# One PSUM tile for the whole kernel, and the last two modulation blocks taken as a pair

## The chip, the cores and the metric

The kernel runs on one core of a Trainium2 chip. The metric is the device time of one execution in microseconds; the median of 3 runs before the change is 1285.03 us (1284.46 to 1285.83). The engines are named as the profile names them: PE (TensorE, matmuls), PEld (its weight loads), DVE (VectorE), ACT (ScalarE), POOL (GpSimd), SP (SyncE, which here only issues transfers).

## What is computed

One layer of a diffusion backbone on 512 tokens of width 2048, with 256 context tokens, cut to what matters here:

```python
shift, scale, gate = split(silu(c) @ w_ada + b_ada, 3)      # 2048 x 6144, one vector each
h = rmsnorm(x, norm_g) * (1 + scale) + shift                # 512 x 2048
p = h @ w_in                                                # 2048 x 9216: q, k, v, z_a, u_b, z_b, g_a, g_b
y_b = (fourier_mix(p[u_b]) * silu(p[z_b])) @ w_pb           # a 2-D FFT, real part, per group of 128 channels
y_a = (attention(q, k, v) * silu(p[z_a])) @ w_pa            # keys and values of the context are appended
out = rmsnorm(x + gate * ((sigmoid(p[g_a]) * y_a + sigmoid(p[g_b]) * y_b) @ w_out), final_g)
```

All is float32. A product is made as three matmuls: each operand is split into a high part and a low remainder (both float32r), and `mm3` (L336 to L340) adds high x high, high x low and low x high into one PSUM bank. A split (`split_from`, L180) is one ACT copy (L181) and one DVE subtraction (L182).

## The kernel before

**Stages.** First comes a start stage, in which the 16 blocks of 128 channels of `h` (the rows `hhi[k]`, `hlo[k]`, 128 channels x 512 tokens each) are made one after another and are used at once for the columns u_b and z_b of `w_in`. The Fourier mixing follows (`tokens`, `positions`, L938 to L963). Then eight groups of 512 x 1024 products of the remaining columns of `w_in` (class `Group`, each of seven products P1, Q5, P2, Q6, P7, Q3, Q4), then attention with the product of `w_pb` filled in between, then the branch and output products.

**How a block of `h` is modulated.** For block k, `modulate(k)` (L573) takes a bank from `bank2` and issues 32 small matmuls (`matvec`, L562: 16 blocks of `c` against a 256-column piece of `w_ada`, on 128 x 32 of the array each, L566). ACT copies the sums out (`taken`, L593). `turned` (L595) transposes them with two matmuls into the other half of the bank (L598). `factors` (L608) adds the quarters with one DVE reduction (L613) and makes gain and shift (L619, L621). `make_h` (L647) scales the row on DVE (L650), makes the high part on ACT (L651) and the low part on DVE (L653). `modulate_pair` (L580) does two blocks in one bank: 64 small matmuls, where the second block's use `c` moved by two columns, then one ACT copy, one pair of transposes and one reduction for both.

**The order in the start stage.** The program writes the order of PE by hand (`manual_schedule(engines={E.PE})`, L796), and until L901 that of ACT and DVE too (L803). The products of the stage come from a generator, `start_work` (L681); `some(n)` takes n of its steps. `STEPS` (L41) says what they are. From block 4 on blocks go in twos: eight steps of one `mm3` (three matmuls of 512 columns) for u_b, the first four with the first block's row, the next four with the second's; then four steps of two `mm3` for z_b. For blocks 12 to 15 it is eight steps of u_b for 12 and 13, then eight for 14 and 15, then z_b of all four. Each u_b piece accumulates in four banks of `bank`; z_b pieces go through the two banks of `bank3` and are added by DVE (L679).

The loop at L863 modulates blocks 6 and 7, 8 and 9, 10 and 11, 12 and 13 in pairs. After the pair 12 and 13 come four steps. The loop at L892 then takes block 14 (two steps, `modulate(14)`, one step, its row) and block 15 (three steps, `modulate(15)`, one step, its row). Row 14 is first used in the ninth step after that loop begins, row 15 in the thirteenth. The pieces of `w_ada` come through SP (`wada_load`, L492): two transfers of 1 MB for a block, into four buffers. The two of block 15 are issued behind the pair 12 and 13.

**PSUM.** There are eight banks. Until the Fourier mixing ends they belong to a pool `ps` with three kinds of tile: `bank` (four), `bank2` (two), `bank3` (two). This pool is closed at L989. The groups then take tiles of two banks from a pool `psp` (`pair`, L1025): tag x with two buffers, y0 and y1. `psp` is closed at L1479, and one tile `whole_psum` with all eight banks follows (L1481), of which attention and all behind it use slices: `wide` for the scores, bank 6 for the products that are filled in (`fill_acc`), bank 7 for the values. A pool that says `reuse_waits="tile"` makes a new tile wait for those old tiles that lie where it lies. Inside one tile an instruction waits for earlier ones that touch the same bank.

**Behind the start stage** the order is not written by hand, except where `issue_after` says so: the compiler's scheduler orders each engine's instructions. The hand-written order of PE ends with the Fourier mixing (L981). `positions(g)` (L950) takes two banks of `bank` for each of four groups: ACT copies the second out (L960), and DVE reads the first twice (L961, L962). The next PE work is P1 of group 0: for each of four pieces of weights two 128-channel blocks times two token blocks t = 0, 1, one bank each (L1101 to L1106).

Of the kernel before, what the change touches and what calls it, by code (L numbers as in the profile page):

```python
# [10 lines left out]
F32 = mybir.dt.float32  # L11
# [4 lines left out]
PSUM = bass.MemoryType.PSUM  # L16
DRAM = bass.MemoryType.DRAM

P = 128
# [3 lines left out]
KK = D // P  # L23
# [100 lines left out]
def block_kernel(ctx, tc, xT, ctx_rows, ctx_toks, x, c_row, w_ss, w_gate, vecs, qkg, rope, dft_c, dft_s,  # L124
# [4 lines left out]
    def region(name, side="left", **kw):  # L129
        st = ExitStack()  # L130
        return st, st.enter_context(tc.tile_pool(name=name, bufs=1, side=side, **kw))
# [18 lines left out]
    b_d = dsc.tile([2, P, 2, T], F32, name="b_d")  # L150
    g_d = dsc.tile([2, 2, 4, P, 1024], F32, name="g_d")
    yb_d = dsc.tile([2, 4, P, 1024], F32, name="yb_d")
    pss, ps = region("ps", None, space=PSUM)

    cnt = [0]

    def uid(s):
        cnt[0] += 1
        return f"{s}{cnt[0]}"
# [8 lines left out]
    def hm_tile(shape, dt, name):  # L168
        return slot(hm, shape[1:], dt)

    def bank(shape=(P, 512)):
        return ps.tile(list(shape), F32, tag="b1", bufs=4, name=uid("pb"))

    def bank2():
        return ps.tile([P, 512], F32, tag="b2", bufs=2, name=uid("pd"))

    def bank3():
        return ps.tile([P, 512], F32, tag="b3", bufs=2, name=uid("pc"))

    def split_from(src, hi, lo):  # L180
        first = nc.scalar.activation(hi, src, ACT.Copy)  # L181
# [302 lines left out]
    def load_start():  # L484

        may[0] = 1
        with tc.issue_after(last_load[0]):
            load_more()
        assert not may[0]
        last_load[0] = asked[0].ins  # L490
# [82 lines left out]
    def modulate(kb, meanwhile=lambda: None):  # L573
        two[kb] = bank2()
        for h in range(2):
            matvec(kb, h)
        meanwhile()
        return taken(kb)

    def modulate_pair(kb, loads):  # L580
        two[kb] = two[kb + 1] = bank2()
        for i in range(2):
            for h in range(2):
                matvec(kb + i, h, i == 0, i == 1)
            if i:
                taken(kb)
            wada.pop(kb + i, None)
            loads(kb + i)
# [13 lines left out]
    def columns(kb):  # L602
        turned(kb)
        factors(kb)
# [42 lines left out]
    def make_h(kb, meanwhile=lambda: None):  # L647
        rows_of(kb)
        v = xt[:, kb, :]
        nc.vector.scalar_tensor_tensor(v, v, gain[:, kb, 0:1], rx if kb else rx0[0], op0=ALU.mult, op1=ALU.mult)  # L650
        act = nc.scalar.activation(hhi[kb], v, ACT.Identity, bias=shift[:, kb, 0:1])  # L651
        meanwhile()
        return nc.vector.scalar_tensor_tensor(hlo[kb], v, shift[:, kb, 0:1], hhi[kb].bitcast(F32),  # L653
                                              op0=ALU.add, op1=ALU.subtract), act

    def form_row(j):

        a, b = xt[:, j, :], xt[:, j + 8, :]
        h, i = divmod(j, 4)
        d = pap.tile([P, 1], F32, tag="d", bufs=2, name=uid("d"))  # L660
        nc.vector.tensor_tensor(d, shift[:, j, 0:1], shift[:, j + 8, 0:1], op=ALU.subtract)
        nc.vector.tensor_tensor(whole["S3", h][:, i, :], a[:, :256], a[:, 256:], op=ALU.subtract)
        nc.vector.scalar_tensor_tensor(whole["Z5", h][:, i, :], a[:, 256:], d, b[:, 256:], op0=ALU.add, op1=ALU.subtract)
# [74 lines left out]
    def some(n):  # L738
        for _ in range(n):
            next(work)  # L740
# [24 lines left out]
    def split_next():  # L765
        e = next(e for e in ahead if e.out is None and e.kind != "raw")
        split_piece(e)
        e.raws = []
# [27 lines left out]
    with tc.manual_schedule(engines={E.PE}):  # L796
        warm(8, ones)
        norms = token_norms()
        two[0] = bank2()
        matvec(0, 0)  # L800
        rx0.append(spread(*norms))
        matvec(0, 1)
        with tc.manual_schedule(engines={E.Activation, E.DVE}):  # L803
            nc.scalar.copy(rx, rx0[0])
            by_root(0)
            split_next()
            taken(0)
            wada[2] = wada_load(2)
            load_start()
            columns(0)  # L810
            row_hi(0)
            scaled(0)
            row_lo(0)
            split_next()
            by_root(1)
            some(4)
            modulate(1)
            rest = split_hi()
            wada[3] = wada_load(3)
            load_start()  # L820
            some(1)
            columns(1)
            some(1)
            row_hi(1)
            rest()
            scaled(1)
            row_lo(1)
            some(2)
            for kb in range(1, 4):
                k = kb + 1  # L830
                some(2 + (kb == 1))
                by_root(k)
                modulate(k, split_next)
                if kb < 3:
                    wada[k + 2] = wada_load(k + 2)
                    load_start()
                hold()
                some(2 - (kb == 1))
                columns(k)
                row_hi(k)  # L840
                release()
                scaled(k)
                if kb < 3:
                    some(2)
                row_lo(k)
                if kb == 3:
                    some(2)
                    by_root(5)
                    modulate(5)
                    for k in (6, 7):  # L850
                        wada[k] = wada_load(k)
                        load_start()
                    hold()
                    some(2)
                    columns(5)
                    row_hi(5)
                    release()
                    scaled(5)
                    load_rope()
                    row_lo(5)  # L860
                else:
                    some(2)
            for kb in range(4, KK - 4, 2):  # L863
                some(3)
                split_next()
                some(5)
                split_next()
                if kb == 6:
                    rotations()
                k = kb + 2  # L870

                def loads(k):
                    wada[k + 2] = wada_load(k + 2)
                    for _ in range(2 if k + 2 == KK - 3 else 1):
                        load_start()

                modulate_pair(k, loads)
                some(1)
                turned(k)
                factors(k)  # L880
                make_h(k, lambda: some(1))
                factors(k + 1)
                make_h(k + 1, lambda: some(1))
                if k >= 8:
                    form_row(k - 8)
                    form_row(k - 7)
                some(1)
                if kb == KK - 6:
                    split_table(0)
                    split_from(get(("dftc", 0)), fch[:, 0, :], fch[:, 1, :])  # L890
                    load_start()
            for k in (KK - 2, KK - 1):  # L892
                some(2 if k < KK - 1 else 3)
                modulate(k)
                some(1)
                columns(k)
                make_h(k)
                split_next()
                if k < KK - 1:
                    load_start()  # L900
                form_row(k - 8)  # L901
        some(1)
        some(8)
    may[0], asks[0] = 1 << 30, nc.sync
    while next(work):
        pass
# [79 lines left out]
    pst.close()  # L986


    pss.close()  # L989
    fm2 = ctx.enter_context(tc.tile_pool(name="fm2", bufs=1, reuse_waits="tile"))  # L990
    fms = [fm] * 4 + [fm2] * (KK - 4)
    turn_fm = [4]
    evs, evp = region("evp", "right", reuse_waits="tile")
    new_ev = lambda: evp.tile([P, 2, 512], F32, tag="ev", bufs=4, name=uid("ev"))
    qzs, qzp = region("qzp", "right", reuse_waits="tile")
    pgs, psp = region("psp", None, space=PSUM, reuse_waits="tile")
    last_y = [0]

    banks = []
    rows4 = lambda hi, lo: [(hi[:, j, :], lo[:, j, :]) for j in range(4)]  # L1000

    def make_form(f, h):
# [22 lines left out]
    def pair(tag, skip=0):  # L1025
        if isinstance(tag, int):
            return banks[0][:, tag : tag + 2, :] if tag < 6 else banks[1]
        if banks:
            last_y[tag == "x"] += 1
            b = 2 * (last_y[tag == "x"] % 2) + (4 if tag == "y" else 0)  # L1030
            return banks[0][:, b : b + 2, :] if b < 6 else banks[1]
        if tag == "y":
            last_y[0] += 1 + skip
            return psp.tile([P, 2, 512], F32, tag=f"y{last_y[0] % 2}", bufs=1, name=uid(tag))
        return psp.tile([P, 2, 512], F32, tag=tag, bufs=2, name=uid(tag))


    forms = {"A11": [(hhi[j][:, :256], hlo[j][:, :256]) for j in range(8)],
# [437 lines left out]
    ats_, atp = region("atp", "right", reuse_waits="tile")  # L1476


    pgs.close()  # L1479
    psq = ctx.enter_context(tc.tile_pool(name="psq", bufs=1, space=PSUM, reuse_waits="tile"))  # L1480
    whole_psum = psq.tile([P, 8, 512], F32, name="banks")  # L1481
    banks += [whole_psum[:, :6, :], whole_psum[:, 6:, :]]
    last_y[:] = [0, 0]
    wide = [flat(banks[0])[:, NKEY * i : NKEY * i + NKEY] for i in range(4)]
    fill_acc, b1 = banks[1][:, 0, :], lambda: banks[1][:, 1, :]
# [605 lines left out]
```

## Time and profile before

| | |
|---|---|
| median of 3 runs | 1285.03 us |
| profiled execution: its time, its span | 1286.17 us, 1284.4 us |
| PE busy | 1269.6 us, 99% |
| DVE, ACT, POOL busy | 77%, 53%, 14% |
| DMA moved | 319.07 MB, mean 248 GB/s |
| instructions | 17614 |

The page of the profile gives busy time by engine and the chain of work that ended last. The timeline lists single instructions: start, duration, engine, line, what is written from what; at the end in brackets how long the engine sat idle before it and what ended that. Matmuls are pipelined: one of 512 columns is shown with 0.39 us, but the next starts about 0.23 us after it. PEld and the bracket of a matmul are therefore read together, and a delay of PE is read from the starts of successive matmuls. In the windows view a row gives busy time by engine in one stretch, and PEclk, the granted clock of TensorE as a share of full speed. In names, pd is a bank of `bank2`, pc of `bank3`, pb of `bank`; ado is the copied sums, wa a piece of `w_ada`.

### The profile page before, as it was taken

Reading aid. Unit: us, or ns where it says so; the run is one execution under the profiler, and the core shown is the slowest. Engines: PE = TensorE matmul, PEld = TensorE weight load, DVE = VectorE, ACT = ScalarE, POOL = GpSimd, SP = SyncE. Lnnn points to the kernel's source line nnn. Section 1 sums busy time; section 2 is a strip of 40 time slices with the busy share of each in tenths; the row PEclk is TensorE's granted clock in tenths of the full one; section 3 lists DMA queues with packets and bytes.
Section 4 is the critical chain, followed back from the end, with each engine's and each line's share of the span. In section 5 each row is a group of like instructions: output and inputs, shape, how many; then the busy total and the mean of one; then the engine's idle time right before and its main releaser. Section 6 shows DMA issues by size and latency. Waiting matters only on the chain.

```text
span 1284.4 us, 17614 instructions
## 1 busy us (share of the span) xinstructions
PE 1269.6 (99%) x6554; PEld 1045.1 (81%) x6554; DVE 989.9 (77%) x1302; ACT 680.9 (53%) x1073; POOL 175.9 (14%) x229
## 2 busy tenths in 40 slices
PE   8999999999999999999999999999999999999997
PEld 5677888888888888888888888888888888788886
DVE  5767899889778787748687656788798777787677
ACT  5322765555456464443354545666677646465544
POOL 0000121111102011012031010021100221211310
PEclk8999999999999999999999999999999999999999
DMA  9998798888898998877879797588762989998986
GB/s 377 405 374 346 244 205 254 229 240 234 236 306 222 299 288 258 290 199 181 285 200 309 234 253 234 174 240 264 250 191 82 249 240 257 247 200 232 218 209 181
DMA packets 104422, 319.07 MB, mean 248 GB/s; under 512 B 9968, under 2 KB 32880, under 8 KB 100368
## 3 DMA queue, kind: packets, MB, share of 16 engines
q1 hardware_dynamic: 54336, 195.24, 42.1%
q0 software_dynamic: 27680, 100.29, 36.8%
q10 hardware_dynamic: 22320, 22.42, 5.1%
q8 instruction: 51, 0.84, 0.2%
q14 instruction: 35, 0.29, 0.1%
HBM read 283.30 MB, written 34.61 MB: 248 GB/s over the span
## 4 chain that ended last, share of the span: by engine, by line
PE 96%; DMA 1%; DVE 1%; ACT 1%; issue 1%; POOL 0%; SPq 0%; DVEq 0%; ACTq 0%
PE banks L338 11%; PE banks L340 10%; PE banks L339 10%; PE x L339 9%; PE x L340 9%; PE x L338 9%; PE y L339 8%; PE y L340 8%; PE y L338 8%; PE banks L1570 3%; PE pd L566 2%; PE pc L338 1%; PE pb L338 1%; PE pc L340 1%; PE pc L339 1%; PE pb L339 1%
## 5 line engine op out<-in xcount | busy, mean ns | idle before, releaser
L181 ACT ACTIVATE whi<-R 128x1024 fp32r<-128x1024 f32 x138 | 145.3, 1058 | 141.7 <-PE banks L340 49.3
L182 DVE TENSOR_TENSOR wlo<-R,whi 128x1024 fp32r<-128x1024 f32 x138 | 168.0, 1223 | 58.9 <-ACT whi L181 58.9
L182 DVE TENSOR_TENSOR wlo<-wr,whi 128x1024 fp32r<-128x1024 f32 (+1 forms) x122 | 147.5, 1215 | 64.5 <-ACT whi L181 64.4
L181 ACT ACTIVATE whi<-wr 128x1024 fp32r<-128x1024 f32 (+1 forms) x122 | 127.2, 1050 | 119.9 <-PE y L340 36.2
L338 PE MATMUL banks<-whi,s 128*128 128x512 f32 (+1 forms) x400 | 157.1, 393 | 0.7 <-ACT ev L1179 0.7
L340 PE MATMUL banks<-whi,s 128*128 128x512 f32 (+1 forms) x400 | 156.3, 391 | 0.0
L339 PE MATMUL banks<-wlo,s 128*128 128x512 f32 (+1 forms) x400 | 156.1, 390 | 0.0
L339 PE MATMUL x<-wlo,s 128*128 128x512 f32 x352 | 137.1, 389 | 0.2 <-DVE wlo L182 0.2
L338 PE MATMUL x<-whi,s 128*128 128x512 f32 x352 | 137.1, 390 | 0.0
L340 PE MATMUL x<-whi,s 128*128 128x512 f32 x352 | 137.0, 389 | 0.0
L291 POOL DMA_DIRECT2D R<-in_w_g x68 | 59.3, 873 | 481.5 <-DVE wlo L182 219.9
L339 PE MATMUL y<-wlo,s 128*128 128x512 f32 x316 | 123.2, 390 | 0.0
L338 PE MATMUL y<-whi,s 128*128 128x512 f32 x316 | 123.0, 389 | 0.0
L340 PE MATMUL y<-whi,s 128*128 128x512 f32 x316 | 122.8, 389 | 0.0
L181 ACT ACTIVATE s<-wr 128x512 fp32r<-128x512 f32 (+2 forms) x93 | 60.4, 676 | 67.0 <-DMA wr<-cf_d 23.9
L182 DVE TENSOR_TENSOR s<-wr,s 128x512 fp32r<-128x512 f32 (+2 forms) x93 | 66.9, 752 | 31.4 <-ACT s L181 30.4
L338 PEld LDWEIGHTS banks<-whi,s 128*128 128x128 f32 x400 | 75.2, 188 | 16.5 <-ACT ev L1179 1.1
L340 PEld LDWEIGHTS banks<-whi,s 128*128 128x128 f32 x400 | 75.2, 188 | 14.9
L339 PEld LDWEIGHTS banks<-wlo,s 128*128 128x128 f32 x400 | 75.2, 188 | 14.0 <-DVE wlo L182 0.2
L339 PEld LDWEIGHTS x<-wlo,s 128*128 128x128 f32 x352 | 66.1, 188 | 14.3 <-DVE wlo L182 0.8
L338 PEld LDWEIGHTS x<-whi,s 128*128 128x128 f32 x352 | 66.1, 188 | 13.7
L340 PEld LDWEIGHTS x<-whi,s 128*128 128x128 f32 x352 | 66.1, 188 | 13.7
(334 smaller groups left out, 2796.2 us busy)
## 6 DMA issues: line engine op xcount, KB each, us to landing
wr<-in_w_g SPq DMA_DIRECT2D x124, 512.0 KB, 5.6
R<-in_w_g POOLq DMA_DIRECT2D x68, 512.0 KB, 7.4
wa<-in_w_ss SPq DMA_DIRECT2D x31, 1024.0 KB, 9.1
R<-in_w_g SPq DMA_DIRECT2D x32, 512.0 KB, 5.6
wr<-in_w_gate SPq DMA_DIRECT2D x32, 512.0 KB, 4.9
wr<-in_w_o SPq DMA_DIRECT2D x24, 512.0 KB, 6.9
R<-in_w_o POOLq DMA_DIRECT2D x24, 512.0 KB, 8.6
wr<-in_w_pab SPq DMA_DIRECT2D x20, 512.0 KB, 5.3
```

Source lines behind the costliest of these rows:

```text
L181: first = nc.scalar.activation(hi, src, ACT.Copy)
L182: return first, nc.vector.tensor_tensor(lo, src, hi.bitcast(F32), op=ALU.subtract)
L291: chained[:] = [nc.gpsimd.dma_start(chain[e.pc], e.nxt, accum_op=ALU.add)]
L338: nc.tensor.matmul(o, ah, bh, start=start, stop=False, skip_group_check=cont)
L339: nc.tensor.matmul(o, ah, bl, start=False, stop=False, skip_group_check=cont)
L340: nc.tensor.matmul(o, al, bh, start=False, stop=stop, skip_group_check=cont)
L566: nc.tensor.matmul(acc[32 * j : 32 * j + 32], c[:, n, :], w[:, k, :], start=first and n < 4, stop=last and n >= KK - 4, skip_group_check=n ...
L1570: nc.tensor.transpose(tp[:, k * P : (k + 1) * P], p[:, k * P : (k + 1) * P], ident)
```

## The change

`whole_psum` is made at the start, the three bank functions take turns over its banks 0 to 3, 4 to 5 and 6 to 7, and `pair` always takes slices of it. In the last part of the start stage the two single blocks become one pair: six steps, the pair's matmuls, one step, transposes, row 14, one step, row 15, one step and so on. The number of steps taken there is sixteen as before. The split and the load that stood behind block 14's row now stand behind the third step.

```diff
-    pss, ps = region("ps", None, space=PSUM)
+    whole_psum = ctx.enter_context(tc.tile_pool(name="ps", bufs=1, space=PSUM)).tile([P, 8, 512], F32, name="banks")
+    in_turn = {}
...
-    def bank(shape=(P, 512)):
-        return ps.tile(list(shape), F32, tag="b1", bufs=4, name=uid("pb"))
+    def turned_bank(first, n):
+        k = in_turn[first] = (in_turn.get(first, -1) + 1) % n
+        return whole_psum[:, first + k, :]
+
+    def bank():
+        return turned_bank(0, 4)
 
     def bank2():
-        return ps.tile([P, 512], F32, tag="b2", bufs=2, name=uid("pd"))
+        return turned_bank(4, 2)
 
     def bank3():
-        return ps.tile([P, 512], F32, tag="b3", bufs=2, name=uid("pc"))
+        return turned_bank(6, 2)
...
-            for k in (KK - 2, KK - 1):
-                some(2 if k < KK - 1 else 3)
-                modulate(k)
-                some(1)
-                columns(k)
-                make_h(k)
-                split_next()
-                if k < KK - 1:
-                    load_start()
-                form_row(k - 8)
-        some(1)
-        some(8)
+            k = KK - 2
+            some(3)
+            split_next()
+            load_start()
+            some(3)
+            modulate_pair(k, lambda k: None)
+            some(1)
+            turned(k)
+            factors(k)
+            make_h(k, lambda: some(1))
+            factors(k + 1)
+            make_h(k + 1, lambda: some(1))
+            split_next()
+            form_row(k - 8)
+            some(1)
+            form_row(k - 7)
+        some(6)
...
-    pss.close()
...
-    pgs, psp = region("psp", None, space=PSUM, reuse_waits="tile")
-    last_y = [0]
-
-    banks = []
+    last_y = [0, 0]
+
+    banks = [whole_psum[:, :6, :], whole_psum[:, 6:, :]]
...
-        if banks:
-            last_y[tag == "x"] += 1
-            b = 2 * (last_y[tag == "x"] % 2) + (4 if tag == "y" else 0)
-            return banks[0][:, b : b + 2, :] if b < 6 else banks[1]
-        if tag == "y":
-            last_y[0] += 1 + skip
-            return psp.tile([P, 2, 512], F32, tag=f"y{last_y[0] % 2}", bufs=1, name=uid(tag))
-        return psp.tile([P, 2, 512], F32, tag=tag, bufs=2, name=uid(tag))
+        last_y[tag == "x"] += 1 + skip
+        b = 2 * (last_y[tag == "x"] % 2) + (4 if tag == "y" else 0)
+        return banks[0][:, b : b + 2, :] if b < 6 else banks[1]
...
-    pgs.close()
-    psq = ctx.enter_context(tc.tile_pool(name="psq", bufs=1, space=PSUM, reuse_waits="tile"))
-    whole_psum = psq.tile([P, 8, 512], F32, name="banks")
-    banks += [whole_psum[:, :6, :], whole_psum[:, 6:, :]]
     last_y[:] = [0, 0]
```

## The prediction

> **What bounds the kernel now.** I read the page first.
>
> ```profile
> PE 1269.6 (99%) x6554; PEld 1045.1 (81%) x6554; DVE 989.9 (77%) x1302; ACT 680.9 (53%) x1073; POOL 175.9 (14%) x229
> ```
>
> PE is busy for 1269.6 of 1284.4 us, so 14.8 us of idle PE are all that can be won by removing waits; for the rest only PE's own work counts, and what holds up its next matmul is added to the time. I therefore price every edit by the starts of successive matmuls in PE's timeline, and look there at the three places that the change touches: the last part of the start stage (108 to 134 us), the place where the groups take over PSUM (153 us), and the place where attention takes it over (803 us). No page view shows these; the timeline by engine does.
>
> **Pairing: what PE saves.** PE's timeline around the pair 12 and 13, and around the single block 14:
>
> ```profile
> 107.86 0.39 PE L339 MATMUL pb<-wlo,s 128*128 128x512 f32 x1
> 108.09 0.39 PE L340 MATMUL pb<-whi,s 128*128 128x512 f32 x1
> 108.41 3.66 PE L566 MATMUL pd<-wa,c 128*32 128x256 f32 x64
> 112.00 0.50 PE L338 MATMUL pc<-s,whi 128*128 128x512 f32 x1
> 112.33 0.40 PE L339 MATMUL pc<-s,whi 128*128 128x512 f32 x1
> ```
>
> ```profile
> 119.04 0.39 PE L340 MATMUL pb<-whi,s 128*128 128x512 f32 x1
> 119.36 1.93 PE L566 MATMUL pd<-wa,c 128*32 128x256 f32 x32
> 121.22 0.50 PE L338 MATMUL pb<-whi,s 128*128 128x512 f32 x1
> 121.56 0.40 PE L339 MATMUL pb<-wlo,s 128*128 128x512 f32 x1
> 121.80 0.40 PE L340 MATMUL pb<-whi,s 128*128 128x512 f32 x1
> 122.03 0.38 PE L598 MATMUL pd<-ident,ado 128*128 128x128 f32 x2
> 122.17 0.48 PE L338 MATMUL pb<-whi,s 128*128 128x512 f32 x1
> 122.48 0.39 PE L339 MATMUL pb<-wlo,s 128*128 128x512 f32 x1
> 122.72 0.40 PE L340 MATMUL pb<-whi,s 128*128 128x512 f32 x1
> ```
>
> Undisturbed matmuls start 0.23 us apart (108.09 - 107.86). The pair pushes the next start from 108.09 to 112.00, 3.91 us, and the start after that is 0.10 late: 3.91 - 0.23 + 0.10 = 3.78 us. A single block takes 121.22 - 119.04 - 0.23 = 1.95, and 0.11 behind it (121.56 - 121.22 = 0.34): 2.06, and two of them 4.12 (block 15 taken like block 14). One pair instead saves 0.34 us. The two transposes stretch three steps of matmuls from 0.69 to 0.92 us (121.80 to 122.72), and one set of them goes: 0.23. **Saved: 0.57 us**, on PE and so on the path. The ACT copy and the DVE reduction that go as well cost no time; both engines wait there.
>
> **Pairing: a transfer that is met earlier.** Block 15's second megabyte of `w_ada` is only just in time now:
>
> ```profile
> 125.16 0.71 PEld L566 LDWEIGHTS pd<-wa,c 128*32 128x32 f32 x16 [0.16 <-DMA wa<-in_w_ss]
> ```
>
> Two steps of three matmuls end at the start 119.04. With no block taken there, four more steps follow: 12 x 0.23 = 2.76, so the pair's first small matmul stands at 119.36 + 2.76 = 122.12. One of them takes 3.59/64 = 0.056 us (112.00 - 108.41), and the last sixteen need that megabyte: 122.12 + 48 x 0.056 = 124.81. It lands at about 125.15, since nothing ahead of it on SP's queue is moved. **Wait: +0.35 us** (0, if it lands earlier, to 0.7).
>
> **Pairing: row 14 has lost its cover.** This is the largest term. Row 14 is needed in the ninth step. Before, block 14 was done after the second; now the pair stands after the sixth, and between its transposes and the ninth step lies one step of three matmuls. What a row takes shows in DVE's and ACT's timelines: first how soon an idle DVE begins the reduction after the transposes start, then the pair 12 and 13 (on DVE the reduction and the low part of row 12, on ACT the high parts of rows 12 and 13).
>
> ```profile
> 44.77 0.38 PE L598 MATMUL pd<-ident,ado 128*128 128x128 f32 x2
> ...
> 45.26 0.17 DVE L613 TENSOR_REDUCE adr<-pd 128x4 f32<-128x16 f32 x1 [1.32 <-PE pd L598]
> ```
>
> ```profile
> 114.42 0.18 DVE L613 TENSOR_REDUCE adr<-pd 128x8 f32<-128x32 f32 x1
> ...
> 116.51 0.75 DVE L653 SCALAR_TENSOR_TENSOR s<-xt,shift,s 128x512 fp32r<-128x512 f32 x1 [0.19 <-ACT s L651]
> ```
>
> ```profile
> 115.75 0.72 ACT L651 ACTIVATE s<-xt,shift 128x512 fp32r<-128x512 f32 x1 [2.85 <-DVE xt L650]
> 118.28 0.72 ACT L651 ACTIVATE s<-xt,shift 128x512 fp32r<-128x512 f32 x1 [1.81 <-DVE xt L650]
> ```
>
> Count from the start of the transposes. The reduction begins at 0.49 (45.26 - 44.77). The high part of the first row ends 115.75 + 0.72 - 114.42 = 2.05 later, at 2.54; its low part ends 116.51 + 0.75 - 114.42 = 2.84 later, at 3.33. PE wants row 14 after one step: 0.92 after the transposes, as 121.80 to 122.72 shows it for three starts, counted from 122.03 to the start that follows 122.72 by 0.23 (122.95). So PE stands from 0.92 to 2.54, makes two matmuls (the second 0.34 later, as after each break above, then 0.23: 3.11), and waits until 3.33 for the low part, which it wanted at 0.92 + 0.46 = 1.38. **Delay: 3.33 - 1.38 = 1.95, with the slow start behind it about +2.0 us.** Row 15 is in time: its high part ends 118.28 + 0.72 - 114.42 = 4.58 behind the reduction, at 5.07, and PE wants it ten matmuls after 3.33, at 3.33 + 0.34 + 9 x 0.23 = 5.74. The order on ACT and DVE is written by hand, with nothing else between these steps, so nothing can be put ahead; `split_next` and `form_row` now stand behind both rows. Bounds: 1.6 (the low part not waited for, PE's start in time) to 2.8 (a split of 1.2 us slips in front).
>
> **One tile: the groups' first banks.** `bank` goes round banks 0 to 3; the four `positions` take 0-1, 2-3, 0-1, 2-3. `pair("x")` starts with its count at 1, which is banks 2-3: those which `positions(3)` has just written. Its readers are one ACT copy (bank 3) and two DVE instructions (bank 2); here are they and the first matmul of P1:
>
> ```profile
> 153.03 0.40 PE L338 MATMUL x<-whi,s 128*128 128x512 f32 x1
> ```
>
> ```profile
> 153.23 0.38 ACT L960 COPY odd<-pb 128x258 f32<-128x258 f32 x1 [0.41 <-PE pb L956]
> ```
>
> ```profile
> 155.54 0.42 DVE L961 TENSOR_TENSOR y<-pb,odd 128x257 f32<-128x257 f32 x1
> 155.87 0.42 DVE L962 TENSOR_TENSOR y<-pb,odd 128x255 f32<-128x255 f32 x1
> ```
>
> Before, P1 started at once, so its tile lay elsewhere. Now token block 0 (bank 2) must wait until 155.87 + 0.42 = 156.29 and token block 1 (bank 3) until 153.23 + 0.38 = 153.61. Nothing else is ready for PE. P1's order is the scheduler's. That it orders by which bank is free is seen in attention, where turn 0's six transposes, two of bank 4 and four of bank 5, were split up, because an ACT read of bank 4 was still to come:
>
> ```profile
> 810.32 0.60 PE L1570 MATMUL banks<-ident,s 128*128 128x128 f32 x4
> 810.68 0.47 PE L338 MATMUL banks<-s,s 128*128 128x512 f32 x1
> ...
> 811.45 0.40 PE L1570 MATMUL banks<-ident,s 128*128 128x128 f32 x2
> ```
>
> ```profile
> 810.37 0.90 ACT L1554 ACTIVATE s<-banks,gain 128x768 f32<-128x768 f32 x1 [1.41 <-DVE gain L1552]
> ```
>
> The two transposes of bank 4 start at 811.45, behind the end of that read at 811.27, and scores went ahead of them. I expect the same of P1: token block 1 first. The two pieces that are ready then give 12 matmuls, 12 x 0.23 = 2.76 us, just what lies between 153.61 and 156.29. **+0.6 us** (153.61 - 153.03; up to 156.29 - 153.03 = 3.3 if the order stays as written; a gain is excluded, PE did not wait there).
>
> **One tile: where attention begins.** The whole tile had to wait for the last reader of the old pool:
>
> ```profile
> 803.17 0.39 PE L340 MATMUL x<-whi,s 128*128 128x512 f32 x1
> 804.23 0.50 PE L338 MATMUL banks<-whi,s 128*128 128x512 f32 x1 [0.68 <-ACT ev L1179]
> ```
>
> ```profile
> 803.59 0.58 ACT L1179 COPY ev<-x 128x512 f32<-128x512 f32 x1 [1.66 <-PE x L340]
> ```
>
> The six matmuls that come first go to bank 6, which last held a y tile, while ACT reads an x tile. With waits by bank they start 0.23 after 803.17: **804.23 - 803.40 = -0.8 us** (0 to -0.9). By then, 1.4 us later, the ACT read is over, so the scores behind them do not wait either.
>
> **Sum:** -0.57 + 0.35 + 2.0 + 0.6 - 0.8 = +1.6 us. The profiled execution took 1286.17, that is 1.8 outside its span and 1.14 above the median; the sum is a difference and goes to both: 1287.8 for a profiled run like it, **1286.6 for the median** of 1285.03. That is +0.12%; 0.2% (2.6 us) is about what a measurement of this kernel can tell from no change.
>
> **Rivals.** (a) *P1 keeps its written order, slower.* Then PE stands 3.3 us at 153 and the sum is +4.3: 1289.3. For it: the swap is the scheduler's guess from its own model of DVE, which I cannot see; DVE is without a break there, so a model that has DVE early returns to bank 2 too soon. Against: the rows at 810. It decides from a wait of 1.6 us on, where the sum passes 2.6. The Trainium skill (PSUM — Partial Sum Buffer, section Engine vs sequencer instructions) says that matmuls start and complete in program order; by that the chip does not mend a bad order, and no row here speaks against it.
>
> (b) *The wait for row 14 costs clock as well, slower.* Once in this trace PE stood long, and the granted clock (the number behind POOL's) fell after it:
>
> ```profile
> 7.17 0.43 PE L547 MATMUL pd<-s,ones 128*32 128x128 f32 x8 [2.35 <-DVE s L545]
> ```
>
> ```profile
> 8.00:12.00 4.00, 3.78 (x26) 1.49 (x28) 2.83 (x5) 3.09 (x6) 0.00 (x0) 0.53 1.02 411
> 12.00:16.00 4.00, 4.00 (x30) 1.79 (x30) 2.93 (x5) 2.49 (x5) 0.00 (x0) 0.61 1.04 415
> ```
>
> That is (0.47 + 0.39) x 4 = 3.4 us of full clock after an idle 2.35. Here the longest wait is 2.54 - 0.92 = 1.6 us, inside dense work. With it the sum is +5.0: 1290.0. The Trainium skill (TensorE: Matmul & The Clock Gate, section Why this matters for your kernels) lets the clock halve only after gaps above about 3 us; by that rule my waits keep it and (a)'s would lose it, for which an estimate from that page's 3.4 us window at half clock is 1.7 us more. The idle 2.35 us above is shorter than its bound, so the trace is not plainly with it.
>
> (c) *Neither new wait shows.* If row 14 is in time and the banks do not collide, what is left is -0.57 - 0.8 = -1.4: 1283.6. Against: the counts above; I see no reason but an error of mine in a step or a bank.
>
> That one tile might tie all banks together is ruled out: behind 804 us the kernel runs on such a tile and PE is busy.
>
> **Chances.** Forecast 0.60, (a) 0.20, (b) 0.06, (c) 0.14. Range 1283.6 to 1289.4: from (c) to (a); the forecast's own, from the bounds of its terms, is 1285.6 to 1288.0. Faster by over 0.2% (under 1282.5) would need more than (c) gives: 0.04. Slower (over 1287.6): (a), (b) and the forecast's upper end, 0.30. Within 0.2%: 0.66.
>
> **What would show it.** In the profile after: L566 once x64 at about 122; an idle PE of about 1.6 us before the first matmul of row 14, ended by ACT L651, with PE a third of a microsecond later waiting on DVE L653; z_b of block 12 (pc) starting 1.8 us later than before; at the groups' beginning 0.6 us of idle PE ended by ACT L960, and matmuls of P1 for one token block first; no wait on ACT L1179. I am wrong if PE does not wait for row 14, or if PE's wait at the groups' start ends with DVE L962.

## The result, and the profile after

The changed kernel takes 1306.72 us (median of 6 runs, 1305.43 to 1308.4), the kernel before, run beside it, 1284.91 us (6 runs, 1283.87 to 1285.83). The ratio is 1.0171, 95% interval 1.0158 to 1.0184: slower by 1.7%, 21.8 us. The forecast was 1286.6 us with a range up to 1289.4, and the measured time lies far outside it.

The profiled execution of the changed kernel has a span of 1304.6 us (20.2 us more) and took 1306.51. The first part of its page:

```profile
PE 1276.2 (98%) x6552; PEld 1047.7 (80%) x6552; DVE 990.8 (76%) x1301; ACT 679.3 (52%) x1072; POOL 171.2 (13%) x229
```

PE is busy 6.6 us longer with two matmuls fewer, and idle 13.6 us longer. That points to waits, and to a lower clock behind them, as the rows below show. In the new file the lines around the change lie 3 to 10 further down (L338 is L343, L651 is L656, L960 is L970, L1128 is L1131, L1179 is L1182), and x, y and pb are all called banks.

To see where the time went, the matmuls of 512 columns, which both kernels have in the same number, are matched one to one in the two PE timelines. The table shows how much the delay of the same matmul grows at each place:

| place (us in the kernel before) | forecast | measured |
|---|---|---|
| last part of the start stage, by 130 | +1.8 | +1.5 |
| groups' start, 155 | +0.6 | +0.8 |
| end of group 0, and its seam to group 1 (205 to 240) | 0 | +1.2, then +5.1 |
| seam from group 1 to 2 (about 308) | 0 | +0.4 |
| groups 2 and 3, the seam between them (360 to 392) | 0 | +0.4, then +10.1 |
| groups 4 to 6 (530 to 660) | 0 | +2.8 |
| attention's start, 804 | -0.8 | -0.8 |

Behind that one step exceeds 0.5 us: at 1121 us 1.3 us come back. The profiles of `e5` and `e13` below, which have the old PSUM pools, show the same against this profile of the kernel before, so it says nothing of the change.

The three places that were forecast came about as forecast. PE's timeline in the start stage of the changed kernel, PE's in the kernel before (one row), then PEld's in the changed kernel:

```profile
121.83 0.39 PE L345 MATMUL banks<-whi,s 128*128 128x512 f32 x1
122.14 3.68 PE L571 MATMUL banks<-wa,c 128*32 128x256 f32 x64
125.75 0.50 PE L343 MATMUL banks<-whi,s 128*128 128x512 f32 x1
...
127.24 0.40 PE L345 MATMUL banks<-whi,s 128*128 128x512 f32 x1
129.15 0.50 PE L343 MATMUL banks<-whi,s 128*128 128x512 f32 x1 [1.52 <-ACT s L656]
...
129.94 0.50 PE L345 MATMUL banks<-whi,s 128*128 128x512 f32 x1
...
135.07 0.39 PE L343 MATMUL banks<-s,whi 128*128 128x512 f32 x1
```

```profile
133.46 0.39 PE L338 MATMUL pc<-s,whi 128*128 128x512 f32 x1
```

```profile
124.75 0.59 PEld L571 LDWEIGHTS banks<-wa,c 128*32 128x32 f32 x16 [0.29 <-DMA wa<-in_w_ss]
...
129.94 0.19 PEld L345 LDWEIGHTS banks<-whi,s 128*128 128x128 f32 x1 [0.49 <-DVE s L658]
```

Row 14 is met too early: its high part ends the wait of 1.52 us, its low part the short one behind it. The rows at 135.07 and 133.46 are the first of z_b of block 12: 1.61 us later, of which 0.07 was there before the place, +1.5.

The second megabyte of block 15 is 0.29 us late for the weight loads. PE does not feel it: from the matmul before the pair to the one behind it (121.83 to 125.75) are 3.92 us, and the pair 12 and 13, which waits for no transfer, takes 3.91.

At the groups' start and at attention's start, again PE, and the ACT copy that PE no longer waits for:

```profile
155.26 0.50 PE L343 MATMUL banks<-whi,s 128*128 128x512 f32 x1 [0.46 <-ACT odd L970]
...
825.36 0.39 PE L345 MATMUL banks<-whi,s 128*128 128x512 f32 x1
825.59 0.39 PE L343 MATMUL banks<-whi,s 128*128 128x512 f32 x1
```

```profile
825.78 0.59 ACT L1182 COPY ev<-banks 128x512 f32<-128x512 f32 x1 [1.66 <-PE banks L345]
```

The loss sits where nothing was forecast, above all at the seams between the first groups. PE, DVE and the windows (us, then busy time of PE, PEld, DVE, ACT and POOL, then the granted clock, DMA share and GB/s) of the changed kernel at the seam from group 2 to group 3:

```profile
391.18 0.39 PE L345 MATMUL banks<-whi,s 128*128 128x512 f32 x1
396.56 1.22 PE L343 MATMUL banks<-whi,s 128*128 128x512 f32 x2 [4.99 <-ACT whi L186]
399.67 0.80 PE L343 MATMUL banks<-s 128*128 128x512 f32 x1 [1.89 <-DVE ev L1131]
400.27 0.63 PE L344 MATMUL banks<-s,s 128*128 128x512 f32 x1
400.69 0.63 PE L345 MATMUL banks<-s,s 128*128 128x512 f32 x1
```

```profile
398.40 1.22 DVE L1131 TENSOR_TENSOR ev<-banks,ev 128x1024 f32<-128x1024 f32 x1
```

```profile
399.00:403.00 4.00, 3.33 (x8) 2.65 (x9) 4.00 (x8) 2.81 (x17) 1.64 (x3) 0.50 0.51 124
403.00:407.00 4.00, 4.00 (x17) 3.20 (x16) 3.61 (x5) 1.53 (x3) 1.98 (x2) 0.84 0.67 115
```

Q4 of group 2 ends with the matmul at 391.18. The next group's P1 starts at 399.67, when DVE has read Q4's sums out (L1131). The two matmuls at 396.56 are no P1: they are the first of the next product, Q5, which the scheduler has put ahead of the blocked P1, and they wait for a split (in `e7` below, where the tiles still have names, the matmul that waits for the split goes to a y tile). The waits are 4.99 + 1.89 = 6.9 us; behind them the matmuls stand 0.43 us apart instead of 0.23, which costs 4 x 0.50 + 4 x 0.16 = 2.6 us more. The same place in the kernel before, PE and DVE:

```profile
381.64 0.39 PE L340 MATMUL x<-whi,s 128*128 128x512 f32 x1
381.86 0.39 PE L338 MATMUL x<-s 128*128 128x512 f32 x1
```

```profile
388.62 1.22 DVE L1128 TENSOR_TENSOR ev<-x,ev 128x1024 f32<-128x1024 f32 x1
```

There too the readout ends 8.2 us after Q4's last matmul (389.84 - 381.64; after: 399.62 - 391.18 = 8.4). But P1 follows Q4 at once, on another tile.

The other two seams have the same collision and a shorter readout. DVE in the kernel before, at the seams from group 0 to 1 and from 1 to 2:

```profile
232.07 1.22 DVE L1128 TENSOR_TENSOR ev<-x,ev 128x1024 f32<-128x1024 f32 x1
...
306.25 1.22 DVE L1128 TENSOR_TENSOR ev<-x,ev 128x1024 f32<-128x1024 f32 x1
```

Q4's last matmuls start at 229.32 and 305.48 there, so the readout ends 4.0 and 2.0 us later. The three seams with 4.0, 2.0 and 8.2 us lost 5.1, 0.4 and 10.1 us: at the second one other matmuls fill the time.

**Theory T1** came from this. A group of the first three uses three x tiles: one for P1 and P2, one for P7 and Q4, and a scratch tile in `qz_done`. The old pool gave P1 a tile that was free. The new `pair` counts turns, and with an odd count per group the next P1 always falls on the two banks that Q4 has just finished. What that costs depends on how late DVE reads them. Rival R1: the start stage ends later, by 1.6 us, and that shifts everything behind it unluckily. Later came R2 and T2, below.

### The profile page after: what moved, and what is told of

It is laid out like the page before. It is cut to its first block, busy times and chain, and to the rows that moved or that the text cites. A ratio compares the mean times of both kernels' runs of the same rounds, so it can differ in the third digit from the quotient of the medians.

```text
span 1304.6 us, 17584 instructions
## 1 busy us (share of the span) xinstructions
PE 1276.2 (98%) x6552; PEld 1047.7 (80%) x6552; DVE 990.8 (76%) x1301; ACT 679.3 (52%) x1072; POOL 171.2 (13%) x229
## 4 chain that ended last, share of the span: by engine, by line
PE 49%; DVE 2%; DMA 1%; ACT 1%; POOL 1%; issue 0%; ACTq 0%; DVEq 0%; SPq 0%; POOLq 0%
PE banks L343 15%; PE banks L344 15%; PE banks L345 15%; PE banks L1569 3%; DMA wr<-in_w_g 1%; DVE wlo L187 1%; PE banks L1683 1%; POOL small L1225 0%; PE banks L1584 0%; PE banks L1418 0%; ACT whi L186 0%; PE banks L1411 0%; ACT banks L1236 0%; DVE qr L1244 0%; DVE wr L282 0%
## 5 line engine op out<-in xcount | busy, mean ns | idle before, releaser
L343 PE MATMUL banks<-whi,s 128*128 128x512 f32 (+1 forms) x1129 | 442.4, 393 | 9.9 <-ACT whi L186 6.2
L344 PE MATMUL banks<-wlo,s 128*128 128x512 f32 (+1 forms) x1129 | 440.9, 391 | 2.7 <-DVE wlo L187 2.6
L345 PE MATMUL banks<-whi,s 128*128 128x512 f32 (+1 forms) x1129 | 440.1, 390 | 0.1
L343 PEld LDWEIGHTS banks<-whi,s 128*128 128x128 f32 x1129 | 212.5, 188 | 57.1 <-ACT whi L186 7.0
L344 PEld LDWEIGHTS banks<-wlo,s 128*128 128x128 f32 x1129 | 212.6, 188 | 46.4 <-DVE wlo L187 4.9
L345 PEld LDWEIGHTS banks<-whi,s 128*128 128x128 f32 x1129 | 212.5, 188 | 43.8 <-DVE s L658 0.5
L344 PE MATMUL banks<-s,s 128*128 128x512 f32 (+1 forms) x444 | 168.9, 380 | 0.7 <-DVE s L187 0.6
L345 PE MATMUL banks<-s,s 128*128 128x512 f32 (+1 forms) x444 | 168.5, 379 | 0.0
L343 PE MATMUL banks<-s,s 128*128 128x512 f32 (+1 forms) x434 | 166.8, 386 | 0.2 <-ACT s L186 0.2
L344 PEld LDWEIGHTS banks<-s,s 128*128 128x128 f32 x444 | 84.1, 189 | 16.4 <-DVE s L187 1.5
L343 PEld LDWEIGHTS banks<-s,s 128*128 128x128 f32 x434 | 81.8, 189 | 18.9 <-ACT s L1553 1.9
L345 PEld LDWEIGHTS banks<-s,s 128*128 128x128 f32 x444 | 84.0, 189 | 15.1
L186 ACT ACTIVATE s<-R 128x512 fp32r<-128x512 f32 (+1 forms) x84 | 54.6, 668 | 33.7 <-PE banks L345 26.2
L187 DVE TENSOR_TENSOR s<-R,s 128x512 fp32r<-128x512 f32 (+1 forms) x84 | 60.2, 737 | 10.8 <-ACT s L186 10.3
L282 DVE TENSOR_TENSOR wr<-R,wr 128x1024 f32<-128x1024 f32 x40 | 48.6, 1219 | 22.3 <-DMA wr<-in_w_g 17.6
```

The source lines that it names most:

```text
L187: return first, nc.vector.tensor_tensor(lo, src, hi.bitcast(F32), op=ALU.subtract)
L282: nc.vector.tensor_tensor(src, chain[e.pc], src, op=ALU.subtract)
L343: nc.tensor.matmul(o, ah, bh, start=start, stop=False, skip_group_check=cont)
L344: nc.tensor.matmul(o, ah, bl, start=False, stop=False, skip_group_check=cont)
L345: nc.tensor.matmul(o, al, bh, start=False, stop=stop, skip_group_check=cont)
```

## The experiments

Each time stands beside runs of the kernel before on the same chip (medians 1284.90, 1284.69 and 1285.18 us in the three sets).

**The turns alone, in the old pools (`e7`).** The kernel before, with its x tiles in turn:

```diff
-    last_y = [0]
+    last_y, turn_x = [0], [0]
...
-        return psp.tile([P, 2, 512], F32, tag=tag, bufs=2, name=uid(tag))
+        turn_x[0] += 1
+        return psp.tile([P, 2, 512], F32, tag=f"x{turn_x[0] % 2}", bufs=1, name=uid(tag))
```

> The kernel before with one difference: the x tiles of its old pool are named x0 and x1 in turn, as the y tiles always were, so that the next group's P1 gets the tile that Q4 has just finished. No one tile and no pair. T1: nearly the whole loss comes back, about 1302 us (1298 to 1306), with waits on the readout ev before P1 of the groups 1 to 3. R1 (late start) and R2 (one tile ties instructions together): 1285 us.

Measured: 1301.0 us, ratio 1.0128 (1.0113 to 1.0143), +16.3 us. PE's timeline has the pair of waits of the changed kernel:

```profile
230.86 0.51 PE L338 MATMUL y<-whi,s 128*128 128x512 f32 x1 [1.20 <-ACT whi L181]
233.64 0.79 PE L338 MATMUL x<-whi,s 128*128 128x512 f32 x1 [2.27 <-DVE ev L1129]
...
393.19 0.80 PE L338 MATMUL y<-whi,s 128*128 128x512 f32 x1 [4.11 <-ACT whi L181]
397.57 0.80 PE L338 MATMUL x<-s 128*128 128x512 f32 x1 [3.58 <-DVE ev L1129]
```

No pair, no one tile, and three quarters of the loss is there. T1 holds.

**The pair undone and the rest of the change kept (`e4`), and the pair alone (`e5`).** `e4` has the loop over blocks 14 and 15 of the kernel before in place of the pair; `e5` is the kernel before with the pair in place of that loop.

> The changed kernel with the pairing alone undone; its one tile and its turns stay. T1 (the turns put the next group's P1 on the banks that Q4 has just finished): the waits for the readout stay, about 1305 us. R1 (the late start stage shifts the rest): about 1284 us.

Measured: 1306.6 us, ratio 1.0161 (1.0137 to 1.0185). The waits are all there with the start stage on time.

> The kernel before with the pair alone, and its old PSUM pools. T1: only the start stage's own cost, the wait for row 14 and for the second transfer less what the pair saves: +1.8 us at 130 us, about 1286.8 us, and nothing more behind it. R1 (the late start shifts the rest unluckily): 1300 us or more.

Measured: 1287.75 us, ratio 1.0021 (1.0012 to 1.003), that is +1.5 to +3.9 us; its start stage costs 1.6 us. R1 falls with these two.

**The turns mended in the changed kernel (`e1`).** The scratch tile takes the banks of the group's own first product and no turn:

```diff
-            e = pair("x" if half else "y")
+            e = group.acc["a"] if half else pair("y")
```

> The changed kernel with one difference: in the first three groups the second scratch tile is put on the banks of the group's own first product (free by then) and no longer takes a turn, so that the next group's P1 never writes the banks that Q4 has just finished. Theory T1 (P1 of the next group waits for DVE's late readout of Q4, because both have the same two banks): the waits on the readout ev before P1 of groups 1, 2 and 3 go, some 17 to 20 us with the clock they cost; about 1287 us, at most 1290. Rival R1 (the start stage ends 1.9 us later, and all transfers and orders behind it are shifted unluckily; banks have no part): about 1306 us as before.

Measured: 1292.23 us, ratio 1.0059 (1.0047 to 1.0071). The waits on the readout are gone, 14.5 us with them, but 1287 was expected. PE now waits for splits; its waits of over 0.5 us between 160 and 800 us:

```profile
208.53 0.50 PE L344 MATMUL banks<-s,s 128*128 128x512 f32 x1 [0.65 <-DVE s L187]
406.89 0.50 PE L344 MATMUL banks<-wlo,s 128*128 128x512 f32 x1 [0.75 <-DVE wlo L187]
528.70 0.50 PE L344 MATMUL banks<-wlo,s 128*128 128x512 f32 x1 [1.38 <-DVE wlo L187]
625.13 0.50 PE L344 MATMUL banks<-wlo,s 128*128 128x512 f32 x1 [0.76 <-DVE wlo L187]
668.70 0.50 PE L344 MATMUL banks<-wlo,s 128*128 128x512 f32 x1 [1.76 <-DVE wlo L187]
```

**One seam mended only (`e6`)**, the same edit for the third group alone:

```diff
-            e = pair("x" if half else "y")
+            e = (group.acc["a"] if group.g == NQZ - 1 else pair("x")) if half else pair("y")
```

> The changed kernel with the scratch tile's turn taken away in the third group alone: the seams from group 0 to 1 and 1 to 2 stay as in the change, the seam from 2 to 3 is free. T1: the wait there goes, 10 us of the 20 with the clock it costs: about 1296.5 us, with the waits at 233 us unchanged. A rival within T1 (a wait that goes at one seam is met at the next one, since the weights are then later): above 1300.

Measured: 1301.74 us, ratio 1.0136 (1.0117 to 1.0156). The step of 10 us at 392 is gone and the one at 235 stays, but half of the gain is given back. In the profile 2.0 us of that stand in the start stage, which this edit does not touch: PE there stands 0.4 us longer for block 15's transfer, and its clock falls behind the wait for row 14 (see the last section). Another 2.4 us stand behind the mended seam: the places from 530 to 660 cost 5.2 us instead of 2.8. The time is that of the rival within T1; its reason, later weights at the next seam, can hold for the second part alone, and no run tests it.

**Other banks for the first P1 (`e2`), and the single blocks back (`e3`).** Both build on `e1`. In `e2` the turns begin on the other two banks; `e3` has blocks 14 and 15 as in the kernel before besides.

```diff
-    last_y = [0, 0]
+    last_y = [0, 1]
```

> As e1_roles, but the turns begin on banks 0-1, so that the first P1 does not meet the banks of the last positions step either. T1: as e1_roles less the 0.5 to 0.8 us that P1 of group 0 waited for ACT at 155 us: about 1286 us. R1: about 1305 us.

> As e2_roles_swapped, with the last two blocks modulated singly as in the kernel before: only the one tile is left of the change, with banks that do not collide. T1: the kernel before less the wait at attention's start, 0.8 us: about 1284 us. R1 (late start): also about 1284, since the start is not late. A rival R2 (one tile ties instructions together that the old pools kept apart, wherever the banks lie): well above 1287.

Measured: 1297.96 us, ratio 1.0108 (1.0095 to 1.0121), and 1292.7 us, ratio 1.0057 (1.0041 to 1.0072; its six runs spread from 1290.03 to 1297.96). Both expectations missed. The wait of P1 at 155 did shrink (0.2 us of delay there instead of 0.8), but more was lost at the same kind of waits as in `e1`. With the single blocks and without a collision the one tile alone costs 5 to 9 us by the interval. So something in it is slow that is neither the turns nor the pair (R2, in some form).

**Theory T2.** I compared the orders of DVE at the end of the kv group (group 5). The kernel before, then `e1`:

```profile
653.45 0.43 DVE L1237 TENSOR_TENSOR y<-ev,qr 128x256 f32<-128x256 f32 x1
...
656.62 2.35 DVE L182 TENSOR_TENSOR wlo<-R,whi 128x1024 fp32r<-128x1024 f32 x2
...
659.49 0.43 DVE L1237 TENSOR_TENSOR y<-ev,qr 128x256 f32<-128x256 f32 x1
```

```profile
662.00 1.44 DVE L1240 TENSOR_TENSOR banks<-ev,qr 128x256 f32<-128x256 f32 x4
...
663.96 1.21 DVE L1243 TENSOR_TENSOR qr<-qr,banks 128x1024 f32<-128x1024 f32 x1
...
666.30 1.22 DVE L1244 TENSOR_TENSOR qr<-qr,small 128x1024 f32<-128x1024 f32 x1
667.43 2.35 DVE L187 TENSOR_TENSOR wlo<-R,whi 128x1024 fp32r<-128x1024 f32 x2
```

These are the steps of `rotated` (L1227): for each token block b, ACT writes squares into the scratch tile, then DVE writes products over them (L1237, in the new file L1240). In the kernel before, the squares of b = 1 wait for the products of b = 0, though they lie in another bank; a row of its ACT timeline shows that release:

```profile
193.56 0.26 ACT L1233 ACTIVATE y<-x 128x128 f32<-128x128 f32 x1 [0.96 <-DVE y L1237]
```

So the tile of two banks was waited for as a whole, and not bank by bank as the section on PSUM says of every tile. Slices of the tile of eight are waited for bank by bank. The squares then run through, all four products follow at once, and the sum and the scaling of the rotation stand on DVE ahead of the splits (wlo), which PE needs sooner. The wait that went had kept the rotation back.

**The same banks in the old tiles (`e11`).** The kernel before with x0 and x1 in turn and the scratch tile as in `e1`:

> The kernel before with its old two-bank tiles, but x0 and x1 named in turn and the scratch tile of the first three groups put on the group's own first product: the same banks for the same products as in e3_one_tile_only, in four tiles of two banks instead of one of eight. Theory T2 (what is left of the loss in e1, e2 and e3 comes from waits that the tile of eight banks no longer asks for: the squares of the second token block on ACT no longer wait for DVE's products of the first, the whole rotation then goes ahead of the splits on DVE, and PE waits for those): the time of the kernel before, 1284 to 1286 us. Rival R3 (the fixed banks themselves cost it): 1290 to 1293 us as e3.

Measured: 1285.5 us, ratio 1.0002 (0.9994 to 1.0011). The fixed banks cost nothing; R3 falls.

**The wait taken out of the kernel before (`e13`).** The squares go where the result will be:

```diff
-                nc.scalar.activation(t2[:, b, h, :], v[:, b, h, :], ACT.Square,
+                nc.scalar.activation(r[:, b, h, :], v[:, b, h, :], ACT.Square,
```

> The kernel before, with the squares of the rotation written where its result will be instead of into the scratch tile, so that the squares of the second token block no longer wait for the products of the first; nothing else. T2: slower than before by 2 to 7 us, with waits for wlo before PE at the ends of the q and k groups. Against T2: within 1 us of before.

Measured: 1290.17 us, ratio 1.004 (1.0027 to 1.0052), +5.0 us. In the profile 4.5 us of it stand at one place, the end of the kv group, and 1.3 us between 390 and 410. The edit does one thing more than take out the wait: the squares now lie where L1235 writes its products, so L1235 follows them. PE, DVE and POOL at the end of the kv group:

```profile
661.82 0.80 PE L339 MATMUL x<-wlo,s 128*128 128x512 f32 x1 [3.25 <-DVE wlo L182]
```

```profile
658.80 0.69 DVE L1322 TENSOR_TENSOR cxe<-cxe,small 128x512 f32<-128x512 f32 x1 [2.58 <-POOL small L1222]
659.41 1.21 DVE L1240 TENSOR_TENSOR qr<-qr,y 128x1024 f32<-128x1024 f32 x1
660.54 1.22 DVE L182 TENSOR_TENSOR wlo<-R,whi 128x1024 fp32r<-128x1024 f32 x1
```

```profile
655.31 2.08 POOL L1222 TENSOR_TENSOR small<-small,mhalf 128x8 f32<-128x8 f32 x1
...
657.76 1.01 POOL L1222 TENSOR_TENSOR small<-small,mhalf 128x4 f32<-128x4 f32 x1
```

The rotation's root (128x8), ready early, goes ahead of that of the context's key (128x4) on POOL. DVE waits 2.58 us for the latter to scale that key, and the split that PE needs stands behind, and behind the rotation's sum as well.

**A like wait put back into the one tile (`e12` from `e2`, `e12b` from `e3`).** In `rotated` both token blocks use the first bank, and the sum is made for each, in two halves instead of one piece (some of the changed lines):

```diff
-                nc.scalar.activation(t2[:, b, h, :], v[:, b, h, :], ACT.Square,
+                nc.scalar.activation(t2[:, 0, h, :], v[:, b, h, :], ACT.Square,
...
+            nc.vector.tensor_tensor(r[:, b], r[:, b], t2[:, 0], op=ALU.add)
...
-        nc.vector.tensor_tensor(r, r, t2, op=ALU.add)
```

> As e2_roles_swapped (one tile, pair), with the rotation's two token blocks made to follow one another: both use the first bank of the scratch tile, and the sum with the products is made for each token block, so that the squares of the second wait for the products and the sum of the first. T2: the waits for wlo before PE at 207, 409, 529 and 669 us shrink or go, 1287 to 1291 us instead of 1298. R4 (what is left has another source in the one tile): 1295 to 1299 us.

> As e3_one_tile_only (one tile, blocks 14 and 15 singly), with the same coupling of the rotation's two token blocks. T2: 1284 to 1288 us instead of 1292.7. R4: 1290 us or more.

Measured: 1290.11 us, ratio 1.0039 (1.0025 to 1.0052), 7.9 us less than `e2`; and 1286.8 us, ratio 1.0019 (1.0011 to 1.0028), 5.9 less than `e3` (medians; `e3` spreads widely). At the end of the kv group `e12` waits 0.17 us where `e2` waits 1.76. At 529 us it still waits 1.62 us, so that wait has another cause. T2 holds for the larger part; neither version beats the kernel before.

**The pair one step earlier (`e8`, from `e2`).**

```diff
-            some(3)
+            some(2)
             modulate_pair(k, lambda k: None)
...
-        some(6)
+        some(7)
```

> As e2_roles_swapped, but the pair stands after five steps instead of six. By the sum on record a step moves 0.69 us from one wait to the other: the wait for row 14 shrinks from about 1.6 to 0.9 us and the one for the second transfer of block 15 grows from about 0.35 to 1.0 us, so the time is that of e2_roles_swapped within 0.4 us. A rival (the transfers are not what is late): 0.7 us less.

Measured: 1297.86 us, `e2` 1297.96. The waits moved as the sum has them. `e2`, then `e8`, each first PEld, then PE:

```profile
124.42 0.59 PEld L571 LDWEIGHTS banks<-wa,c 128*32 128x32 f32 x16 [0.28 <-DMA wa<-in_w_ss]
```

```profile
128.84 0.50 PE L343 MATMUL banks<-whi,s 128*128 128x512 f32 x1 [1.52 <-ACT s L656]
```

```profile
124.85 0.59 PEld L571 LDWEIGHTS banks<-wa,c 128*32 128x32 f32 x16 [0.98 <-DMA wa<-in_w_ss]
```

```profile
129.25 0.50 PE L343 MATMUL banks<-whi,s 128*128 128x512 f32 x1 [0.84 <-ACT s L656]
```

The wait for the row fell by 0.68 us, the one for the transfer grew by 0.70. At five steps PE does feel the transfer: it stands still for 0.50 us itself, and the pair takes 4.62 us between its neighbours instead of 3.91.

## Why the prediction was wrong

**The pair (-0.57 + 0.35 + 2.0 = +1.8).** The waits are those forecast, each ended by the engine named, and the sum came to +1.5. Row 14 cost what was forecast: its low part is used at 129.94, and without a wait that would be 127.24 + 3 x 0.23 = 127.93, 2.0 us earlier (forecast 1.95). The +0.35 for the transfer was too much: the loads waited 0.29 us, PE next to nothing (3.92 us against 3.91). The trace of before shows it too: the loads of block 15 waited 0.16 us there, and PE took 126.28 - 124.10 = 2.18 us, as for block 14 (121.22 - 119.04). The step of `e8` confirms that both waits are there and are traded against each other.

**The groups' first banks (+0.6), attention's start (-0.8).** Right: +0.8, with ACT's copy as the end of the wait, and -0.8. Twelve matmuls follow that copy before DVE's last read there ends (158.21), so token block 1 came first. Rivals (a) and (c) did not happen. Rival (b) did not happen in this execution, whose clock stayed at 1.00 through the wait for row 14; of the six profiles with this wait two show it, those of `e6` and `e12` (last section). That it stayed out here was luck, and its chance of 0.06 was low.

**The step that failed** is the sum's account of the one tile. It has two terms, the place where the groups take over PSUM and the place where attention does. Between them the prediction takes the new turns to give the same tiles as the pool did. It followed `pair("x")` to its first tile ("its count at 1, which is banks 2-3") and not to the fourth. Counting on would have shown it: banks 2-3, 0-1, 2-3 in group 0, and P1 of group 1 on 0-1, which Q4 has just left. The price could be read in the trace of before, in the 4.0, 2.0 and 8.2 us between Q4's last matmul and the end of L1128. In the runs the turns are worth 16.3 us put in alone, 14.5 us taken out.

**A second term was missing**, 5 to 8 us (+5.0 when its wait is taken out of the kernel before, -7.9 and -5.9 when a like one is put back; the intervals of these times are 2 to 4 us wide). The prediction asked only whether one tile might tie banks together, and rightly ruled that out. It did not ask what waits the old tiles had made that the new one leaves out; the one such wait that it looked at, at attention's start, was a gain. Here a wait also set the order: in the kernel before POOL makes the root of the context's key at 654.95 and that of the rotation at 663.23, in `e13` at 657.76 and 655.31.

What the prediction named as its own tests (PE waits for row 14; the wait at the groups' start does not end with DVE) both came out its way. They looked only at places that were already in the sum.

**Open:** about 1.2 us at 207 us is in every run with the tile of eight banks, with the coupling too, and in none with the old tiles. DVE is without a break there, and its order differs in several places at once. Also open is why `e2` loses 5.7 us on `e1`: its waits are of the same kind, but no run separates them.

## What to carry to other kernels

Before a pool that gives out whatever is free is replaced by a fixed turn, write down the turn through one whole loop, and set against each reuse the time until the last reader is done. An odd number of uses per loop with two buffers moves the clash onto the next loop's first product. And where a coarse wait goes, look at what it kept back on the other engines: work that becomes ready early can go ahead of what the bound engine needs.

## What was unexpected of the hardware

The same wait costs clock in one execution and not in another. The wait of 1.52 us for row 14 stands in the profiles of the changed kernel, `e1`, `e2`, `e5`, `e6` and `e12`, with PE busy for 2.42 to 2.48 us of the four us from 126 to 130 in all six. The next four us in the changed kernel, in `e6` and in `e12`:

```profile
130.00:134.00 4.00, 4.00 (x18) 3.30 (x19) 3.01 (x7) 2.62 (x3) 0.00 (x0) 1.00 0.02 4
```

```profile
130.00:134.00 4.00, 3.95 (x12) 3.13 (x12) 3.02 (x8) 2.62 (x3) 0.00 (x0) 0.63 0.01 5
```

```profile
130.00:134.00 4.00, 4.00 (x13) 3.12 (x12) 3.02 (x6) 2.62 (x3) 0.00 (x0) 0.58 0.03 9
```

In `e1`, `e2` and `e5` the clock stays at 1.00 there, as in the changed kernel. In `e6` and `e12` it falls, which costs about 1.7 us of full clock each (0.37 x 4, and 0.05 x 4 in the four us behind, in `e6`; 0.42 x 4 in `e12`). A single wait of 1.76 us (`e1` at 668 us) left it at 1.00. At the first seam of the changed kernel two waits, 1.20 and 1.75 us, with two matmuls between them, were followed by a lower clock (windows of that kernel):

```profile
233.00:237.00 4.00, 1.11 (x4) 0.30 (x2) 3.97 (x5) 1.06 (x1) 0.00 (x0) 1.00 0.88 257
237.00:241.00 4.00, 3.94 (x10) 3.16 (x11) 3.97 (x9) 2.46 (x16) 2.20 (x3) 0.57 0.68 169
```

That is 0.43 x 4 = 1.7 us on top of 2.95 us of waits. The Trainium skill (TensorE: Matmul & The Clock Gate, section Why this matters for your kernels) warns of idle gaps above about 3 us between bursts of matmuls. Here shorter ones were followed by a lower clock, 1.52 us the shortest. What decides whether a wait of this length costs clock is not shown by these runs.
